# Turning a query tile's maxima into rows of the key product: four small products and one wide step, or one product and four narrow steps

## The chip, the cores and the metric

The kernel runs on one core of a Trainium2 chip. Its time is the device time of one execution in microseconds (us); several executions are timed and their median is compared. The core has TensorE (PE, matrix products; PEld is its weight load), VectorE (DVE), ScalarE (ACT), GpSimd (POOL) and SyncE (SP, which here only issues transfers). Each engine takes its instructions in order; semaphores tie the engines together.

## The reference

One step of a decoder trunk for a prompt of 2048 tokens and 8 samples of 4 tokens. Both share the weights. A layer is a normalisation, one wide input projection, an attention branch (A), a gated recurrence (B), a gated merge of both, an output projection and a residual. The change lies in branch A of the prompt, which attends in three ways: to 127 compressed blocks, to the 8 best blocks of 64 keys, and to a window of 512 keys. For the selected blocks and the window:

```
ss = einsum('bgrtd,bgtnsd->bgrtns', qg, ksg) + bias_s      # selected
ps = masked_softmax(ss, ms)
sw = einsum('bgrtd,blgd->bgrtl', qg, kw) + table[:, :, t5_bucket(rel_w)]
o_win = einsum('bgrtl,blgd->bgrtd', masked_softmax(sw, mw), vw)
```

There are 2 key heads (g) with 4 query heads (r) each. A softmax may subtract any number per query and head before the exponential; the kernel subtracts a maximum, so that the exponential stays in range. The bias differs from key to key only within some 112 positions of the query; beyond that it is one value.

## The kernel before

Everything up to about 1430 us is projections, compression, the samples' attention and the recurrence. `attention_setup` then builds constants, and `prompt_phase` runs the prompt's attention and, beside it, the remaining projections (`pfill`) and the merge with its output projection (`block`, handed out in small parts by `fill`).

The prompt's queries are cut in 16 tiles of 128. `run_block` takes one tile at a time in the order `ORDER`. A unit is a tile and a key head. Logits are computed transposed, 128 keys by 4 x 128 queries, by `score`: two or more products into one PSUM tile `st` (L1633, biases at L1639 and L1640 or L1642, and L1643). The maximum has to be subtracted along the queries, so it is put into extra rows of the query operand `qs` (rows 96 on) that meet constant rows of the key operand `kas` or `kw`. `probs` then takes the exponential twice on ScalarE (L1432 in 32 bits, L1433 in 16 bits), GpSimd takes their difference (L1434), and `pv` multiplies with the values (L1440, L1441, L1443). While one tile is attended to, the maxima of the next one are found (`max_ops`) and the compressed part of the one after (`prep`).

`max_ops` computes the untransposed logits of up to 4 key tiles per PSUM tile `mx` (L1518), adds the near bias by products with a flipped identity (L1520), one for the query's own key tile (128 columns) and one for the tile before it (112 columns), adds the window's far edge in the same way, and reduces over the keys on VectorE (L1521). `last` reduces over the chunks and, after the selected branch, calls `neg_row`.

`neg_row` takes maxima as 128 queries x 4 heads x n (n is 2 for selected and window together, 1 for the compressed branch), splits them in two 16-bit halves in `xd` (L1420, L1421), turns each head's 2n columns into 2n rows by a product with the identity into its quarter of the PSUM tile `tr` (L1424, four products of 128 columns), and writes all 4 x 128 queries in one ScalarE step with a bias per row (L1426). It is called once per unit for the selected branch (out `qs`) and once for the compressed branch (out `qc`): 64 calls, 4 for each query tile. `tr` has one buffer, which `sel` (L1584) and `finish` (L1660) use too.

The order of the work is written out in `run_block`: lists A (maxima of the next tile) and B (compressed part of the one after) are spread over the key tiles of the present one, and `fill` adds merge work by credit. Tile's scheduler then plans each engine's order from the dependencies and its own timeline (`TC_ARGS`). The first two tiles' compressed parts and the first tile's maxima are done ahead of the loop, from about 1430 us on, between pieces of `pfill`; this stretch is called the lead-in below.

Of the kernel before, what the change touches and what calls it, by code (L numbers as in the profile page):

```python
# [10 lines left out]
F32 = mybir.dt.float32  # L11
# [42 lines left out]
def shape_constants():  # L54
# [46 lines left out]
    c["shift"] = (np.arange(256)[None, :] + np.arange(16)[:, None] == 127).astype(np.float32)  # L101
    kb = np.zeros((36, 2048), np.float32)
    kb[:32] = (np.arange(2048)[None, :] // 64 == np.arange(32)[:, None]) * 2.0 ** 15
    kb[32:36:2] = 1024.0
    c["kblk"] = kb
    wone = np.zeros((36, 256), np.float32)
    wone[33::2] = 1024.0
    c["wone"] = wone
    c["edge"] = np.where(rows[:, None] > rows[None, :], 0.0, -60000.0).astype(np.float32)
    c["edgeq"] = c["edge"].T.copy()  # L110
# [18 lines left out]
def trunk_kernel(ctx: ExitStack, tc: tile.TileContext, A, O):  # L129
# [1112 lines left out]
    def attention_setup(st, a):  # L1242

        pc_ = st.enter_context(tc.tile_pool(name="pc", bufs=1, side="right"))
        with tc.tile_pool(name="ps0", bufs=2, side="right") as p0, tc.tile_pool(name="ps0p", bufs=1, space=PSUM, side="right") as p0p:
# [28 lines left out]
            ve.tensor_mul(swb, swb, tw)  # L1274
            nb = con.tile([4, 2], F32, name="nb")
            ve.memset(nb, LN_P * QS / 1024)
            for n in (1, 2):
                ve.memset(nb[:n, n - 1:n], 0.0)
            ve.tensor_scalar(gates[:, :16], gates[:, :16], vsc, None, op0=OP.mult)
            a.update(nb=nb, sk=sk, sv=sv, vsc=vsc, swa=swa, swb=swb, swo=swo, u2=u2)  # L1280

# [33 lines left out]
            t_ = p0.tile([128, 512], F32, name="cl")  # L1315
            sy.dma_start(t_[64:100, :256], A["c_wone"])
            a["wone"] = pc_.tile([100, 256], F16, name="wone")
            ve.tensor_copy(a["wone"][64:100], t_[64:100, :256])

# [6 lines left out]
            for g in range(2):  # L1326
                h0 = g * 4 * 2 * BRN
                for dl in range(2):
# [9 lines left out]
                    tq = pc_.tile([128, 4, 128], F16, name=f"tq{g}{dl}")  # L1338
                    ve.tensor_copy(tq, rq)
                    a["TQ"][g, dl] = tq  # L1340
# [13 lines left out]
            for g in range(2):  # L1354
                ka = pc_.tile([98, 128], F16, name=f"kac{g}0")
                k2 = pc_.tile([98, 128], F16, name=f"kac{g}1")
                kb = pc_.tile([128, 128], F16, name=f"kbc{g}")
                ve.tensor_scalar(ka[:64], kcp[:, g], sk[:64], None, op0=OP.mult)
                ve.memset(ka[96:98], 1024.0)
                ve.tensor_copy(k2[:64], ka[:64])  # L1360
                ve.memset(k2[96:98], 1024.0)
# [13 lines left out]
            for g in range(2):  # L1375
                KA["s", g] = pc_.tile([100, NP], F16, name=f"kas{g}")
                KB["s", g] = pc_.tile([128, NP], F16, name=f"kbs{g}")
            V["s"] = pc_.tile([128, 16, 2, 129], F16, name="vs16")
            ve.memset(V["s"][:, :, :, 64:65], 1.0)
            for c in range(4):  # L1380
                cs = slice(c * 512, (c + 1) * 512)
                bl = p0.tile([100, 512], F32, name="bl")
                sy.dma_start(bl[64:100], A["c_kblk"][:, cs])
                for g in range(2):
                    ka, kb = KA["s", g], KB["s", g]
                    kr = p0.tile([128, 512], F32, name="qr")
                    for h in range(2):
                        sy.dma_start(kr[h * 64:(h + 1) * 64], ks_d[g * 64:(g + 1) * 64, cs])
                    ac.activation(kb[:, cs], kr, AF.Copy, scale=sk)
                    ve.tensor_copy(ka[:64, cs], kb[:64, cs])  # L1390
                    ve.scalar_tensor_tensor(kb[:64, cs], kr[:64], sk[:64], ka[:64, cs], op0=OP.mult, op1=OP.subtract)
                    ve.tensor_copy(ka[64:100, cs], bl[64:100])
# [13 lines left out]
    def prompt_phase(a, st, pfill, state, sw):  # L1406
# [9 lines left out]
        def neg_row(m, dst):  # L1416

            n = m.shape[2]
            x = pu.tile([128, 4, 4], F16, name="xd")[:, :, :2 * n]
            ve.tensor_scalar(x[:, :, :n], m, -1.0 / 1024, None, op0=OP.mult)  # L1420
            ve.scalar_tensor_tensor(x[:, :, n:], m, -1.0 / 1024, x[:, :, :n], op0=OP.mult, op1=OP.subtract)  # L1421
            pt = ptr.tile([128, 4, 128], F32, name="tr")
            for r in range(4):
                mm(pt[:2 * n, r], x[:, r], a["id"], r == 0, True)  # L1424

            ac.activation(dst, pt[:2 * n], AF.Identity, bias=a["nb"][:2 * n, n - 1:n], scale=1.0 / QS)  # L1426

# [20 lines left out]
        def window(c):  # L1448
            cs = slice(c * 256, (c + 1) * 256)
            for g in range(2):  # L1450
                kr = pu.tile([128, 256], F32, name="kr", bufs=1)
                for h in range(2):
                    sy.dma_start(kr[h * 64:(h + 1) * 64], kw_d[g * 64:(g + 1) * 64, cs])
                ka = pu.tile([100, 256], F16, name=f"kw{g}", bufs=4)
# [4 lines left out]
                ve.tensor_copy(ka[64:100], a["wone"][64:100])  # L1459
                KW[c, g], KX[c, g] = ka, kb  # L1460
# [16 lines left out]
        def loads(t, g, turn):  # L1477
            u = {"k": KA["c", g][turn]}
            q0 = t * 128
            for nm, n in (("s", 100), ("c", 98), ("b", 128)):  # L1480
                u[nm] = pu.tile([n, 4, 128], F16, name="q" + nm, bufs={"c": 2}.get(nm, 6))
# [6 lines left out]
        def max_ops(u, br, t, g):  # L1488

            qq, K, k0 = u["s"], 96, 0 if br == "s" else max(0, t - 4)  # L1490
            nt = t + 1 - k0
            nch = (nt + 3) // 4
            mp_ = pu.tile([128, 4, 4], F32, name="mp" + br, bufs=3)
# [3 lines left out]
            def one(c, r):  # L1497
                ka, kz = k0 + c * 4, min(k0 + c * 4 + 4, t + 1)
                n = (kz - ka) * 128
                pm = pmx.tile([128, 4, 128], F32, name="mx")  # L1500
                pmf = flat(pm)
                sp_ = []
                for kt in (t, t - 1):
                    if ka <= kt < kz:
                        w0 = 0 if kt == t else 129 - FAR
                        sp_.append((a["flip"], TQ[g, t - kt][:, r, w0:], kt - ka, w0))
                if br == "w" and t >= 4 and ka <= t - 4 < kz:
                    sp_.append((a["id"], a["edgeq"], t - 4 - ka, 0))
                if br == "s":
# [7 lines left out]
                for i, (x, y, kk) in enumerate(runs):  # L1517
                    mm(pmf[:, (x - ka) * 128:(y - ka) * 128], qq[:K, r], kk, i == 0, not sp_)  # L1518
                for i, (l, rr, kk, w0) in enumerate(sp_):
                    mm(pm[:, kk, w0:], l, rr, False, i == len(sp_) - 1)  # L1520
                ve.tensor_reduce(mp_[:, r, c:c + 1], pmf[:, :n], axis=AX.X, op=OP.max)  # L1521

            def last():
                ve.tensor_reduce(u["m"][:, :, "sw".index(br)], mp_[:, :, :nch], axis=AX.X, op=OP.max)
                if br == "s":
                    neg_row(u["m"], u["s"][96:100])

# [13 lines left out]
        def prep(u, t, g):  # L1541
# [44 lines left out]

            return [cmax, lambda: neg_row(X["m"][:, :, None], u["c"][96:98]), cs, cpv, sel]

# [429 lines left out]
```

## Time and profile before

| | |
|---|---|
| runs shown | 2498.12, 2499.87, 2505.35 us, median 2499.87 |
| the profiled execution's own time | 2498.46 us |
| its span in the trace | 2496.1 us |
| instructions | 57172, of these 22228 products and as many weight loads |

The profile is of one execution. A row of a timeline gives the start, the time taken, the engine, the line and what is written from what; "x4" stands for several in a row that were merged, and the idle time before with what ended it stands in brackets. The time from one start to the next on PE is what a product costs in a stream; the time of one product includes its way through the array. ACT, DVE and POOL rows give what one instruction takes.

### The profile page before, as it was taken

The page shows a single profiled execution, that of the slowest core. Times are in us where ns is not written, and L with a number is a line of the kernel's source. Part 1 is how long each engine was busy: PE and PEld are TensorE (multiplying, and loading weights), DVE is VectorE, ACT ScalarE, POOL GpSimd, SP SyncE. Part 2 cuts the span into 40 slices and gives each one's busy share as a digit, 9 for nine tenths or more (in the row PEclk, how much of TensorE's full clock was granted, in tenths as well). Part 3 has the DMA queues.
Part 4 walks back from the last instruction along what each step waited for, and adds up shares of the span by engine and source line. Part 5 has one row for each costly group of instructions (what it writes and reads, how often), then busy time and mean ns, then how long its engine had stood idle before and what let it go on. Part 6 is the DMA issues. An engine that isn't in the chain of part 4 may idle for free.

```text
span 2496.1 us, 57172 instructions
## 1 busy us (share of the span) xinstructions
PE 2357.9 (94%) x22228; PEld 1554.0 (62%) x22228; DVE 1575.8 (63%) x4232; ACT 1198.0 (48%) x2639; POOL 989.9 (40%) x1179
## 2 busy tenths in 40 slices
PE   5999999998999999999989969899999999999998
PEld 4988675554785555555555446656666666565765
DVE  7556455656325688777763667677777767767543
ACT  5544333422223366555552346436555666667763
POOL 0100102332102255444550006536656666677864
PEclk9999999999999999999999979999999999999999
DMA  6543314656322434333323652322222221211121
GB/s 202 170 121 115 121 69 163 218 205 217 131 65 105 144 105 132 115 118 97 109 87 98 192 159 63 79 81 69 78 58 72 57 66 51 63 52 45 48 59 46
DMA packets 266719, 264.96 MB, mean 106 GB/s; under 512 B 95100, under 2 KB 237872, under 8 KB 259280
## 3 DMA queue, kind: packets, MB, share of 16 engines
q1 hardware_dynamic: 257936, 223.56, 29.0%
q0 software_dynamic: 8512, 37.75, 4.6%
q8 instruction: 175, 2.87, 0.5%
q14 instruction: 96, 0.79, 0.1%
HBM read 181.84 MB, written 83.55 MB: 106 GB/s over the span
## 4 chain that ended last, share of the span: by engine, by line
PE 68%; DVE 14%; DMA 7%; ACT 4%; issue 4%; POOL 1%; SPq 1%; DVEq 0%; ACTq 0%; POOLq 0%
PE ps L361 14%; PE ps L440 9%; PE ps L1786 7%; PE ps L1754 6%; PE ps L421 4%; PE st L1643 3%; PE st L1633 3%; PE mx L1518 3%; DVE X L683 2%; DMA wraw<-in_w_in_dram 2%; PE ph L920 2%; PE po L1440 2%; PE po L1443 2%; PE po L1441 2%; DVE mps L1521 1%
## 5 line engine op out<-in xcount | busy, mean ns | idle before, releaser
L1434 POOL TENSOR_TENSOR Pl<-P,Ph 128x512 f16<-128x512 f32 (+5 forms) x444 | 516.6, 1173 | 406.8 <-ACT Ph L1433 171.6
L1432 ACT ACTIVATE P<-st 128x512 f32<-128x512 f32 (+3 forms) x444 | 264.6, 596 | 204.8 <-PE st L1643 157.5
L361 PEld LDWEIGHTS <-wh 128*128 128x128 f16 x2240 | 214.3, 99 | 190.4 <-issue 45.2
L1433 ACT ACTIVATE Ph<-st 128x512 f16<-128x512 f32 (+5 forms) x444 | 262.6, 593 | 14.9 <-PE po L1441 10.8
L361 PE MATMUL ps<-xh,wh 128*128 128x512 f16 (+1 forms) x1120 | 234.5, 344 | 11.0 <-DVE row L374 5.1
L1521 DVE TENSOR_REDUCE mps<-mx 128x1 f32<-128x512 f32 (+3 forms) x320 | 189.2, 605 | 75.9 <-PE mx L1518 45.7
L361 PE MATMUL ps<-xl,wh 128*128 128x512 f16 (+1 forms) x1120 | 236.0, 347 | 1.1 <-issue 1.0
L361 PE MATMUL ps<-xh,wl 128*128 128x512 f16 (+1 forms) x1120 | 232.3, 341 | 0.0
L440 PE MATMUL ps<-wh,xh 128*128 128x256 f16 (+3 forms) x680 | 189.4, 279 | 7.0 <-ACT to L447 4.3
L440 PE MATMUL ps<-wh,xl 128*128 128x256 f16 (+3 forms) x680 | 188.4, 278 | 4.0 <-DVE xl L327 4.0
L440 PE MATMUL ps<-wl,xh 128*128 128x256 f16 (+3 forms) x680 | 189.0, 278 | 0.0
L1440 PEld LDWEIGHTS <-Ph 128*128 128x128 f16 (+5 forms) x1776 | 138.8, 98 | 41.3 <-issue 6.9
L361 PEld LDWEIGHTS <-wl 128*128 128x128 f16 x1120 | 107.9, 98 | 86.3 <-issue 9.4
L1441 PEld LDWEIGHTS <-Ph 128*128 128x128 f16 (+5 forms) x1776 | 128.7, 96 | 32.7 <-issue 1.4
L440 PEld LDWEIGHTS <-xh 128*128 128x128 f16 (+1 forms) x1360 | 129.9, 99 | 30.7 <-issue 6.5
L686 POOL TENSOR_TENSOR X<-X,kt 128x128 f32<-128x128 f32 x160 | 81.8, 512 | 142.8 <-ACT X L685 142.8
L1521 DVE TENSOR_REDUCE mpw<-mx 128x1 f32<-128x512 f32 (+3 forms) x224 | 104.9, 485 | 49.6 <-PE mx L1520 46.7
L652 POOL TENSOR_TENSOR Xo<-Xo,qt 128x256 f32<-128x256 f32 x32 | 30.5, 953 | 260.4 <-ACT Xo L651 229.3
L1754 PEld LDWEIGHTS <-xh 128*128 128x128 f16 x1280 | 105.3, 98 | 30.3 <-issue 9.1
L1518 PE MATMUL mx<-kas,qs 96*128 96x512 f16 (+3 forms) x320 | 109.8, 355 | 10.4 <-DVE mps L1521 7.7
L1443 PEld LDWEIGHTS <-Pl 128*128 128x128 f16 (+3 forms) x1776 | 96.1, 97 | 30.9 <-POOL Pl L1434 8.4
L1440 PE MATMUL po<-vs,Ph 128*128 128x65 f16 x1088 | 106.6, 192 | 0.8 <-DVE otmp L1535 0.8
(538 smaller groups left out, 5918.9 us busy)
## 6 DMA issues: line engine op xcount, KB each, us to landing
wraw<-in_w_in_dram SPq DMA_DIRECT2D x22, 1024.0 KB
xt<-in_x_prompt_dram SPq DMA_DIRECT2D x32, 512.0 KB
ma_d<-row SPq DMA_DIRECT2D x8, 1040.0 KB
out_y_prompt_dram<-xt SPq DMA_DIRECT2D x16, 512.0 KB
sg<-ma_d SPq DMA_DIRECT2D x56, 128.0 KB
sg<-mb_d SPq DMA_DIRECT2D x56, 128.0 KB
mb_d<-row SPq DMA_DIRECT2D x18, 256.0 KB
q_d<-row SPq DMA_DIRECT2D x4, 1040.0 KB
```

Source lines behind the costliest of these rows:

```text
L361: mm(ps, l[:, kc], xs(r, t0, n)[:, kc], k == 0, k == 23)
L440: mm(ps, xs(l, t0, r)[:, kc], w[:, kc], k == 0, k == 23)
L1432: ac.activation(P[:n], ps, AF.Exp, scale=1.0 / QS)
L1433: ac.activation(ph[:n], ps, AF.Exp, scale=1.0 / QS)
L1434: sub.tensor_sub(pl[:n], P[:n], ph[:n])
L1440: mm(po[:, r, :w], ph[:n, rs[r]], v[:n, :w], first and r == 0, False)
L1441: mm(po[:, r, :64], ph[:n, rs[r]], v[:n, w:w + 64], False, False)
L1443: mm(po[:, r, :w], pl[:n, rs[r]], v[:n, :w], False, last)
L1518: mm(pmf[:, (x - ka) * 128:(y - ka) * 128], qq[:K, r], kk, i == 0, not sp_)
L1521: ve.tensor_reduce(mp_[:, r, c:c + 1], pmf[:, :n], axis=AX.X, op=OP.max)
L1754: mm(X["ps"], w[:, kc, cs], os_[o][:, kc], k == 0, k == 11)
L1786: mm(X["ps"], X["y"][y][:, kc, i0:i0 + r], W["o", kc // 4][w][:, kc % 4, cs], k == 0, k == 23)
```

## The change

The four products of `neg_row` become one: `xd` is laid out head by head, all 8n columns are turned into 8n rows at once, and each head has its own 2n of these rows, separate from the other heads'. The query operand gets 4 x 2n rows in place of 2n (`qs` 96 to 112, `qc` 96 to 104); in the 128 queries of head r only head r's rows hold numbers and the others are zero. Four ScalarE steps write them, one per head, each reading all 8n rows and taking a scale and a bias per row from the constant `own` (zero for rows of other heads). The key operands get matching constant rows (`c_kblk`, `c_wone`, the `memset` of `kac`). `own` comes by one transfer in place of three `memset`s of `nb`.

In `max_ops` the two bias tiles `tq` of a key head become one tile of 240 columns, and the two products with the flipped identity become one, over the last 240 columns. For that the chunks are cut so that a query's own key tile and the one before it always lie in one chunk: where a tile would have stood alone at the end it now takes the one before with it, and the five window tiles are cut as 3 and 2 or 2 and 3 in place of 4 and 1. The number of chunks stays.

```diff
-            x = pu.tile([128, 4, 4], F16, name="xd")[:, :, :2 * n]
-            ve.tensor_scalar(x[:, :, :n], m, -1.0 / 1024, None, op0=OP.mult)
-            ve.scalar_tensor_tensor(x[:, :, n:], m, -1.0 / 1024, x[:, :, :n], op0=OP.mult, op1=OP.subtract)
-            pt = ptr.tile([128, 4, 128], F32, name="tr")
+            x = pu.tile([128, 16], F16, name="xd")[:, :8 * n]
+            xv = x.rearrange("p (r k) -> p r k", r=4)
+            ve.tensor_scalar(xv[:, :, :n], m, -1.0 / 1024, None, op0=OP.mult)
+            ve.scalar_tensor_tensor(xv[:, :, n:], m, -1.0 / 1024, xv[:, :, :n], op0=OP.mult, op1=OP.subtract)
+            pt = ptr.tile([128, 4, 128], F32, name="tr")[:8 * n, 0]
+            mm(pt, x, a["id"], True, True)
+            own = a["own"][:8 * n, 2 - n]
             for r in range(4):
-                mm(pt[:2 * n, r], x[:, r], a["id"], r == 0, True)
-
-            ac.activation(dst, pt[:2 * n], AF.Identity, bias=a["nb"][:2 * n, n - 1:n], scale=1.0 / QS)
+                ac.activation(dst[:, r], pt, AF.Identity, bias=own[:, 4 + r:5 + r], scale=own[:, r:r + 1])
...
-            nch = (nt + 3) // 4
+            cut = [min(x, t - 1) for x in range(k0 + 4, t + 1, 4)]
+            if br == "w" and cut:
+                cut = [t - 1 - (t - 1) % 2]
+            cut = [k0, *cut, t + 1]
+            nch = len(cut) - 1
...
-                ka, kz = k0 + c * 4, min(k0 + c * 4 + 4, t + 1)
+                ka, kz = cut[c:c + 2]
...
-                for kt in (t, t - 1):
-                    if ka <= kt < kz:
-                        w0 = 0 if kt == t else 129 - FAR
-                        sp_.append((a["flip"], TQ[g, t - kt][:, r, w0:], kt - ka, w0))
-                if br == "w" and t >= 4 and ka <= t - 4 < kz:
-                    sp_.append((a["id"], a["edgeq"], t - 4 - ka, 0))
+                if kz > t:
+                    w = 127 + FAR if t else 128
+                    sp_.append((a["flip"], TQ[g][:, r, 127 + FAR - w:], n - w, n))
+                if br == "w" and t >= 4 and ka == t - 4:
+                    sp_.append((a["id"], a["edgeq"], 0, 128))
...
-            nb = con.tile([4, 2], F32, name="nb")
-            ve.memset(nb, LN_P * QS / 1024)
-            for n in (1, 2):
-                ve.memset(nb[:n, n - 1:n], 0.0)
+            own = con.tile([16, 2, 8], F32, name="own")
+            sy.dma_start(own.rearrange("p i r -> p (i r)"), A["c_own"])
...
-                    neg_row(u["m"], u["s"][96:100])
+                    neg_row(u["m"], u["s"][96:112])
...
-            return [cmax, lambda: neg_row(X["m"][:, :, None], u["c"][96:98]), cs, cpv, sel]
+            return [cmax, lambda: neg_row(X["m"][:, :, None], u["c"][96:104]), cs, cpv, sel]
```

## Rows read from the trace of the kernel before

**Rows 1.** First part of the page: busy us, share of the span, instructions.

```profile
PE 2357.9 (94%) x22228; PEld 1554.0 (62%) x22228; DVE 1575.8 (63%) x4232; ACT 1198.0 (48%) x2639; POOL 989.9 (40%) x1179
```

**Rows 2.** Windows, two stretches: length, busy us (instructions) per engine, clock, DMA, GB/s.

```profile
1430.00:1600.00 170.00, 138.71 (x1487) 87.51 (x1486) 116.89 (x395) 85.92 (x157) 66.62 (x71) 0.88 0.38 103
1600.00:2400.00 800.00, 782.21 (x8646) 522.65 (x8645) 560.07 (x1498) 472.04 (x919) 509.63 (x493) 0.98 0.22 62
```

**Rows 3.** Timeline of PE, two places in a dense stretch.

```profile
2079.87 0.27 PE L1520 MATMUL mx<-tq,h_flip 128*128 128x128 f16 x2
2079.98 0.19 PE L1440 MATMUL po<-vs,Ph 128*128 128x65 f16 x1
...
2315.31 0.39 PE L1424 MATMUL tr<-h_id,xd 128*4 128x128 f16 x4
2315.63 0.40 PE L1518 MATMUL mx<-kw,qs 96*128 96x128 f16 x3
```

**Rows 4.** Lines L1520 and L1424, ns min/median/max; the last from 1600 to 2400 alone.

```profile
L1520 PEld LDWEIGHTS <-h_flip x496: 95/98/152, 1475.0 to 2382.4; 128*128 128x128 f16 x166
L1424 PEld LDWEIGHTS <-xd x256: 79/83/129, 1438.8 to 2389.2; 128*2 128x2 f16 x64, 128*4 128x4 f16 x64
...
L1424 PE MATMUL tr<-h_id,xd x192: 217/218/314, 1601.8 to 2389.2; 128*4 128x128 f16 x104, 128*2 128x128 f16 x88
```

**Rows 5.** Groups of ACT by shape: count, busy us, mean ns, idle before, releaser.

```profile
L1432 ACT ACTIVATE P<-st 128x512 f32<-128x512 f32 x412 | 245.7, 596 | 189.5 <-PE st L1643 157.5 <-POOL Pl L1434 23.9 <-PE po L1443 2.3
L1763 ACT ACTIVATE yh<-pr 128x256 f16<-128x256 f32 x56 | 23.4, 417 | 36.4 <-POOL pr L1761 36.2
L1426 ACT ACTIVATE qs<-tr,nb 4x512 f16<-4x512 f32 x32 | 21.7, 677 | 61.4 <-PE tr L1424 61.1
L748 ACT ACTIVATE jk<-ov 128x128 bf16<-128x128 f32 x64 | 16.9, 275 | 0.0
L1456 ACT ACTIVATE kx<-kr,sk 128x256 f16<-128x256 f32 x16 | 8.1, 506 | 14.2 <-DMA kr<-kw_d 12.4 <-PE st L1633 1.7
```

**Rows 6.** Timeline of ACT where one query tile gives way to the next.

```profile
1892.37 0.68 ACT L1426 ACTIVATE qs<-tr,nb 4x512 f16<-4x512 f32 x1 [7.44 <-PE tr L1424]
1893.94 0.68 ACT L1426 ACTIVATE qs<-tr,nb 4x512 f16<-4x512 f32 x1 [0.90 <-PE tr L1424]
1894.65 0.60 ACT L1432 ACTIVATE P<-st 128x512 f32<-128x512 f32 x1
1895.14 0.59 ACT L1433 ACTIVATE Ph<-st 128x512 f16<-128x512 f32 x1
```

**Rows 7.** Timeline of PE at the same place.

```profile
1891.75 0.58 PE L1424 MATMUL tr<-h_id,xd 128*4 128x128 f16 x4
...
1893.32 0.58 PE L1424 MATMUL tr<-h_id,xd 128*4 128x128 f16 x4
1893.84 1.03 PE L1643 MATMUL st<-qs,kw 100*128 100x512 f16 x2
...
1896.72 0.19 PE L1440 MATMUL po<-vw,Ph 128*128 128x65 f16 x1
```

**Rows 8.** Windows: ahead of this place, round it, and round the last like it.

```profile
1665.00:1885.00 220.00, 218.04 (x2432) 146.40 (x2431) 162.94 (x457) 130.91 (x256) 140.54 (x138) 1.00 0.26 71
1885.00:1900.00 15.00, 13.13 (x124) 8.85 (x122) 12.62 (x37) 6.08 (x12) 5.89 (x6) 0.77 0.35 109
...
2160.00:2175.00 15.00, 13.25 (x109) 8.34 (x106) 12.87 (x34) 5.67 (x11) 4.76 (x6) 0.77 0.08 19
```

**Rows 9.** Waits of the whole program, PE: us in total, times, longest.

```profile
PE mx L1518 <- DVE mpw L1521: 8.6, 10, 1.8
PE mx L1518 <- DVE mps L1521: 8.3, 18, 2.4
```

**Rows 10.** Groups of DVE by shape, the reductions over one chunk.

```profile
L1521 DVE TENSOR_REDUCE mpw<-mx 128x1 f32<-128x512 f32 x104 | 69.9, 685 | 12.6 <-PE mx L1520 12.0
L1521 DVE TENSOR_REDUCE mpw<-mx 128x1 f32<-128x128 f32 x104 | 27.7, 287 | 36.5 <-PE mx L1520 34.3 <-PE po L1443 1.4
```

More of the change, by code (lines that the diff above doesn't have):

```diff
@@ L101, in shape_constants @@
     c["shift"] = (np.arange(256)[None, :] + np.arange(16)[:, None] == 127).astype(np.float32)
-    kb = np.zeros((36, 2048), np.float32)
+    kb = np.zeros((48, 2048), np.float32)
     kb[:32] = (np.arange(2048)[None, :] // 64 == np.arange(32)[:, None]) * 2.0 ** 15
-    kb[32:36:2] = 1024.0
+    kb[32::2] = 1024.0
     c["kblk"] = kb
-    wone = np.zeros((36, 256), np.float32)
+    wone = np.zeros((48, 256), np.float32)
     wone[33::2] = 1024.0
     c["wone"] = wone
+    own = np.zeros((16, 2, 8), np.float32)
+    for i, n in enumerate((2, 1)):
+        p = np.arange(8 * n)
+        own[:8 * n, i, :4] = (p[:, None] // (2 * n) == np.arange(4)[None, :]) / QS
+        own[:8 * n, i, 4:] = own[:8 * n, i, :4] * (p // n % 2)[:, None] * (LN_P * QS / 1024 * QS)
+    c["own"] = own.reshape(16, 16)
     c["edge"] = np.where(rows[:, None] > rows[None, :], 0.0, -60000.0).astype(np.float32)
@@ L1274, in attention_setup @@
             ve.tensor_mul(swb, swb, tw)
-            nb = con.tile([4, 2], F32, name="nb")
-            ve.memset(nb, LN_P * QS / 1024)
-            for n in (1, 2):
-                ve.memset(nb[:n, n - 1:n], 0.0)
+            own = con.tile([16, 2, 8], F32, name="own")
+            sy.dma_start(own.rearrange("p i r -> p (i r)"), A["c_own"])
             ve.tensor_scalar(gates[:, :16], gates[:, :16], vsc, None, op0=OP.mult)
-            a.update(nb=nb, sk=sk, sv=sv, vsc=vsc, swa=swa, swb=swb, swo=swo, u2=u2)
+            a.update(own=own, sk=sk, sv=sv, vsc=vsc, swa=swa, swb=swb, swo=swo, u2=u2)
             OSh = p0.tile([64, 8, 32], F16, name="OSh", bufs=1)
@@ L1315, in attention_setup @@
             t_ = p0.tile([128, 512], F32, name="cl")
-            sy.dma_start(t_[64:100, :256], A["c_wone"])
-            a["wone"] = pc_.tile([100, 256], F16, name="wone")
-            ve.tensor_copy(a["wone"][64:100], t_[64:100, :256])
+            sy.dma_start(t_[64:112, :256], A["c_wone"])
+            a["wone"] = pc_.tile([112, 256], F16, name="wone")
+            ve.tensor_copy(a["wone"][64:112], t_[64:112, :256])
             brt = br_d.tensor
@@ L1327, in attention_setup @@
                 h0 = g * 4 * 2 * BRN
+                tq = a["TQ"][g] = pc_.tile([128, 4, 127 + FAR], F16, name=f"tq{g}")
                 for dl in range(2):
@@ L1337, in attention_setup @@
                     sy.dma_start(rq, toep(h0 + BRN + (BRN - 1 - BR0) - 127 - 128 * dl, [[1, 128], [2 * BRN, 4], [1, 128]]))
-                    tq = pc_.tile([128, 4, 128], F16, name=f"tq{g}{dl}")
-                    ve.tensor_copy(tq, rq)
-                    a["TQ"][g, dl] = tq
+                    if dl:
+                        ve.tensor_copy(tq[:, :, :FAR - 1], rq[:, :, 129 - FAR:])
+                    else:
+                        ve.tensor_copy(tq[:, :, FAR - 1:], rq)
                     yield
@@ L1354, in attention_setup @@
             for g in range(2):
-                ka = pc_.tile([98, 128], F16, name=f"kac{g}0")
-                k2 = pc_.tile([98, 128], F16, name=f"kac{g}1")
+                ka = pc_.tile([104, 128], F16, name=f"kac{g}0")
+                k2 = pc_.tile([104, 128], F16, name=f"kac{g}1")
                 kb = pc_.tile([128, 128], F16, name=f"kbc{g}")
                 ve.tensor_scalar(ka[:64], kcp[:, g], sk[:64], None, op0=OP.mult)
-                ve.memset(ka[96:98], 1024.0)
+                ve.memset(ka[96:104], 1024.0)
                 ve.tensor_copy(k2[:64], ka[:64])
-                ve.memset(k2[96:98], 1024.0)
+                ve.memset(k2[96:104], 1024.0)
                 ve.scalar_tensor_tensor(kb[:64], kcp[:, g], sk[:64], ka[:64], op0=OP.mult, op1=OP.subtract)
@@ L1375, in attention_setup @@
             for g in range(2):
-                KA["s", g] = pc_.tile([100, NP], F16, name=f"kas{g}")
+                KA["s", g] = pc_.tile([112, NP], F16, name=f"kas{g}")
                 KB["s", g] = pc_.tile([128, NP], F16, name=f"kbs{g}")
@@ L1381, in attention_setup @@
                 cs = slice(c * 512, (c + 1) * 512)
-                bl = p0.tile([100, 512], F32, name="bl")
-                sy.dma_start(bl[64:100], A["c_kblk"][:, cs])
+                bl = p0.tile([112, 512], F32, name="bl")
+                sy.dma_start(bl[64:112], A["c_kblk"][:, cs])
                 for g in range(2):
@@ L1391, in attention_setup @@
                     ve.scalar_tensor_tensor(kb[:64, cs], kr[:64], sk[:64], ka[:64, cs], op0=OP.mult, op1=OP.subtract)
-                    ve.tensor_copy(ka[64:100, cs], bl[64:100])
+                    ve.tensor_copy(ka[64:112, cs], bl[64:112])
                     yield
@@ L1453, in window @@
                     sy.dma_start(kr[h * 64:(h + 1) * 64], kw_d[g * 64:(g + 1) * 64, cs])
-                ka = pu.tile([100, 256], F16, name=f"kw{g}", bufs=4)
+                ka = pu.tile([112, 256], F16, name=f"kw{g}", bufs=4)
                 kb = pu.tile([128, 256], F16, name=f"kx{g}", bufs=4)
@@ L1458, in window @@
                 ve.scalar_tensor_tensor(kb[:64], kr[:64], a["sk"][:64], ka[:64], op0=OP.mult, op1=OP.subtract)
-                ve.tensor_copy(ka[64:100], a["wone"][64:100])
+                ve.tensor_copy(ka[64:112], a["wone"][64:112])
                 KW[c, g], KX[c, g] = ka, kb
@@ L1479, in loads @@
             q0 = t * 128
-            for nm, n in (("s", 100), ("c", 98), ("b", 128)):
+            for nm, n in (("s", 112), ("c", 104), ("b", 128)):
                 u[nm] = pu.tile([n, 4, 128], F16, name="q" + nm, bufs={"c": 2}.get(nm, 6))
@@ L1518, in one @@
                     mm(pmf[:, (x - ka) * 128:(y - ka) * 128], qq[:K, r], kk, i == 0, not sp_)
-                for i, (l, rr, kk, w0) in enumerate(sp_):
-                    mm(pm[:, kk, w0:], l, rr, False, i == len(sp_) - 1)
+                for i, (l, rr, x, y) in enumerate(sp_):
+                    mm(pmf[:, x:y], l, rr, False, i == len(sp_) - 1)
                 ve.tensor_reduce(mp_[:, r, c:c + 1], pmf[:, :n], axis=AX.X, op=OP.max)
```

## The prediction

> **What bounds the kernel now.** I read the page's first part, then windows by stage, the groups by shape of the instructions touched, and timelines of places where a tile's maxima become rows. TensorE (PE) is busy for 94% of the span [rows 1]. The changed code runs only behind 1430 us, in two kinds of time [rows 2]. From 1600 to 2400 us PE is busy for 782 of 800 us, with a granted clock of 0.98: here a product less is time saved, and a longer step on another engine costs only where PE runs out of other work. From 1430 to 1600 us, the lead-in, PE is busy for 139 of 170 us: here chains through VectorE, ScalarE and transfers set the pace.
>
> The dense stretch isn't even. From 1665 to 1885 us PE is busy for 218 of 220 us at clock 1.00. Round 1892 us it is busy for 13.1 of 15 us at a mean clock of 0.77, so part of it at the lower of two levels, while VectorE is busy for 12.6 [rows 8]. There a query tile ends, the timeline has no product of the merge, and ScalarE stands idle for 7.4 us until the product of `neg_row` releases it [rows 6]. Three more changes of tile look like this one, the last round 2168 us [rows 8]. At these four a longer `neg_row` has least to hide behind.
>
> **The change part by part, in us.**
>
> *One product for four.* In the dense stretch the four take 0.32 from the first start to the next line's start [rows 3]. Two flipped products of 128 and 112 columns take 0.11 in the same stretch, so 128 columns cost about 0.055. Three products less save 0.165. 192 of the 256 products, 48 calls, lie behind 1600 [rows 4]: 48 x 0.165 = 7.9 saved. Bounds: the four cost 0.10 more than their columns; if that went too, 0.265 a call, 12.7. Where PE waits anyway the saving is nothing. I take 7.9, since the narrow weights that come with the 0.10 stay, 16 wide in place of 4.
>
> *One flipped product for two.* 240 per run of the program go (15 tiles, 2 heads, 2 branches, 4 query heads; 496 weight loads [rows 4] become 256). The columns stay: 240 x 0.055/128 is 0.103 against 0.11. 240 x 0.007 = 1.7 saved, bounds 0 and the rival below.
>
> *The cuts.* A window row's reductions took 685 ns (512 columns) and 287 (128) [rows 10], 1.04 a column. 384 and 256 columns are 554 and 420 by that: 972 before, 974 behind. VectorE's load stays; nothing, bounds in the rivals.
>
> *Four ScalarE steps for one.* No row shows a step with 128 columns and both scale and bias from a tile, so I build it. The old step took 677 ns with 512 columns [rows 5]. A column costs (596 - 275)/384 = 0.836 ns, from L1432 and L748, so 384 fewer leave 356. A scale taken from a tile costs 506 - 417 = 89 more (L1456 against L1763): 445. Then the queue: P and Ph overlap, Ph starts 0.49 behind P though P takes 0.60, but the old step overlaps with nothing: P starts at 1894.65, 0.03 behind its end [rows 6]. It writes from partition 96 on as the new ones do, so I give each 24 ns more: 4 x 0.469 = 1.88 against 0.70, 1.18 more a call. Bounds: four steps of 275 that overlap by 0.10 cost 0.70, nothing more; four of 506 with the gap cost 2.12, 1.42 more. The sum over 64 calls is 76 us of ScalarE, busy for 472 of 800 in the dense stretch; as load that fits, so it counts only as lateness.
>
> The Trainium skill (page "ScalarE: Activation LUTs", section "What ACT_TABLE_LOAD costs") gives 186 ns plus 0.833 a column, some 93 for each scale or bias from a tile, and says that steps back to back overlap by about 93. By that page four steps are an estimated 1.64 us. Its slope agrees with the 0.836 here; its overlap does not with L1426's 0.03 gap, and the row decides. By the page a call adds 0.94 and not 1.18, and the lateness below is some 1.5 less in all.
>
> *Lateness at the four bare changes of tile.* Taken from 1892 [rows 6, 7], where the clock's lower level (1.2 of 2.4 GHz) makes 128 columns twice 0.055, 0.11. The first ScalarE step starts 0.62 behind the first product; three products less make that 0.29, so the four run from 1892.04 to 1893.92, where the one ended at 1893.05. `tr` has one buffer: the second head's product, at 1893.32 now, waits until some 1893.94, and PE's queue stands behind it. The scores (L1643) started 0.52 behind it, now 0.19: 1894.13, 0.29 later than now. The second head's steps run from 1894.23 to 1896.11, and P starts at 1896.13 in place of 1894.65, 1.48 late. Ph ended at 1895.73 and PE took it at 1896.72: 0.99 is cover. Left are 0.49, with the 0.29 in them: 4 x 0.49 = 2.0 lost. Bounds: 0 if P is planned between the two calls, 4 x 1.5 = 6.0 if the cover is used up elsewhere.
>
> *Lateness at the other changes of tile and in the compressed branch.* Their two calls lie further apart than one call now lasts, so one call's 1.18 falls on a tile, less 0.165 that the product ends sooner: 1.0 against a cover of 0.99. I take 1.0 in all, bounds 0 and 40 x 1.0.
>
> *Lead-in.* 16 calls, while PE lies idle for 31 of 170 us [rows 2]. That is a fifth of the time, so I let three calls (a fifth) show in full, 1.0 each as above: 3.0. Bounds 0 and 16.
>
> *Setup.* One small transfer for three memsets and 12 more constant rows, beside PE's projections: nothing.
>
> Sum: -7.9 - 1.7 + 2.0 + 1.0 + 3.0 = -3.6, which makes the profiled execution's 2498.46 some 2494.9. The median of the runs lies 1.4 above that execution, so the forecast is 2496.3, 0.14% less than 2499.87. What this kernel's runs can tell from no change is about 0.3%, 7.5 us: 2492.4 to 2507.4 counts as the same.
>
> **The rivals.**
>
> *Slower: `tr`'s single buffer.* The place is every change of tile, not four. PE stands behind the second head's product, P behind eight ScalarE steps instead of two. With no cover, 15 changes cost 1.5 each, 22.5, and the lead-in 3.0; less 9.6 saved that is +15.9, 2515.8; with 0.4 of cover at each it is 15 x 1.1 + 3.0 - 9.6 = +9.9, 2509.8. It decides for slower from 0.94 a change on, (7.5 + 9.6 - 3.0)/15. For it: ScalarE's idle rows at L1426, 61.1 us in all [rows 5], say that it often comes last. Against: PE has 218 of 220 us of work around most of them [rows 8].
>
> *Faster: PE stops waiting for VectorE.* L1518 waits 16.9 us for reductions [rows 9], since `mx` has two buffers. Chunks of 2 and 3 instead of 4 and 1 might free buffers more evenly: half of it, 8.4, on top of 9.6 with the lateness hidden, gives 2499.9 - 18.0 = 2481.9. Against: VectorE's sum is the same, and where it is the bound an even cut gives nothing.
>
> *Faster: weight loads set PE's pace.* Loads of 98 and 83 ns [rows 4] would go with each product: 240 x 0.098 + 192 x 0.083 = 39.5, less 6.0 lateness: 2466.4. Against: two flipped products with two loads took 0.11 [rows 3], less than 0.196; loads overlap.
> The Trainium skill (page "TensorE: Matmul & The Clock Gate", section "Back-to-back issue gap") states about 81 ns for a 128-column product with its load in a real stream, which points the same way; 0.055 here speaks against it.
>
> *The change doesn't do what it says*: the planner could put the four steps apart, with other work between, so that the rows are complete later still. It ends as the first rival and is counted there.
>
> **How the numbers follow.** Forecast 0.49, between 2489 and 2505 by itself; `tr` and its like 0.25, even VectorE 0.22, weight loads 0.04. The faster rivals make 0.26 faster, the first rival 0.25 slower, and 0.49 is within 0.3%. The range for 8 in 10 reaches into both sides: down to 2484, where 6.3 of the 8.4 us of waits for VectorE are gone, and up to 2511, just past the slower rival with 0.4 of cover; this leaves out about 1 in 10 at either end.
>
> **What would show it.** L1424 with 64 products and L1520 with 352 (256 flipped, 96 edges); PE's product count lower by some 430 to 480. L1426 with 256 steps of about 445 ns, the four 0.47 apart and without overlap; at 300 ns or with overlap the ScalarE term is wrong. The second L1424 at the four changes of tile 2.2 or more behind the first, with PE idle ahead of it and ACT's `tr` as releaser; if the pair stands as before, the lateness is wrong. L1518's wait for L1521 still near 17 us; if it is halved, the second rival has it. ScalarE's busy time up by 70 us with PE's idle time in 1600 to 2400 unchanged within 5 us shows that the load was hidden. Wrong would be any change beyond 7.5 us.

## The result, and the profile after

The changed kernel takes 2523.04 us (median of 6 runs, 2515.94 to 2526.09) against 2501.27 us of the kernel before on the same chip (6 runs, 2495.87 to 2509.05): 1.0086 of its time, 95% interval 1.0071 to 1.01. The forecast was 2496.3 us and no change that can be told; it is slower, and outside the range.

The profiled execution took 2524.28 us, its span 2522.2. First the engines' part of the page, in the form of [rows 1]:

```profile
PE 2359.4 (94%) x21748; PEld 1546.1 (61%) x21748; DVE 1558.8 (62%) x4229; ACT 1247.1 (49%) x2831; POOL 993.8 (39%) x1179
```

TensorE has 480 products fewer, of which the forecast's sum counted 432 (the other 48 are key products of the maxima, L1532, that the new cuts save), and is busy for 1.5 us longer. The windows show where, in the columns of [rows 2]:

```profile
1430.00:1600.00 170.00, 131.52 (x1321) 79.07 (x1320) 102.27 (x364) 95.29 (x201) 65.06 (x69) 0.86 0.35 98
1600.00:2400.00 800.00, 768.03 (x8117) 507.33 (x8116) 547.64 (x1508) 495.61 (x1036) 502.62 (x483) 0.97 0.21 61
2400.00:2522.00 122.00, 108.99 (x1237) 72.72 (x1234) 45.01 (x139) 58.99 (x129) 65.26 (x69) 0.95 0.17 50
```

From 1600 to 2400 TensorE does 8117 products where it did 8646, and is idle for 32 us instead of 18. So the work is not heavier; it is done more slowly, and what isn't done by 2400 is done behind it.

The groups by shape (the view of [rows 5] and [rows 10], behind 1430 us) of the new product, the new steps and the even window cuts:

```profile
L1535 DVE TENSOR_REDUCE mpw<-mx 128x1 f32<-128x384 f32 x104 | 55.9, 550 | 44.2 <-PE mx L1534 43.8
...
L1436 ACT ACTIVATE qs<-tr,own 16x128 f16<-16x128 f32 x128 | 47.4, 438 | 48.4 <-PE tr L1433 48.1
L1436 ACT ACTIVATE qc<-tr,own 8x128 f16<-8x128 f32 x128 | 47.3, 438 | 3.2 <-PE tr L1433 2.5
...
L1535 DVE TENSOR_REDUCE mpw<-mx 128x1 f32<-128x256 f32 x104 | 42.2, 417 | 18.4 <-PE mx L1534 17.5
...
L1433 PE MATMUL tr<-h_id,xd 128*16 128x128 f16 x32 | 7.5, 233 | 1.1 <-DVE qs L1599 0.4 <-ACT qs L1436 0.2 <-DVE oo L1686 0.2
L1433 PE MATMUL tr<-h_id,xd 128*8 128x128 f16 x32 | 7.2, 225 | 3.1 <-ACT qc L1436 2.0 <-DVE qs L1599 1.2
```

A step takes 438 ns (forecast 445) and a reduction 550 and 417 (554 and 420). Then the change of tile of [rows 6], now at 1907 us; the timeline of ScalarE:

```profile
1907.20 1.48 ACT L1436 ACTIVATE qs<-tr,own 16x128 f16<-16x128 f32 x4 [8.49 <-PE tr L1433]
1909.04 1.48 ACT L1436 ACTIVATE qs<-tr,own 16x128 f16<-16x128 f32 x4 [0.35 <-PE tr L1433]
1910.54 0.60 ACT L1442 ACTIVATE P<-st 128x512 f32<-128x512 f32 x1
```

and of all engines, in excerpt:

```profile
1906.89 0.28 PE L1433 MATMUL tr<-h_id,xd 128*16 128x128 f16 x1
...
1908.73 0.27 PE L1433 MATMUL tr<-h_id,xd 128*16 128x128 f16 x1
1908.93 1.03 PE L1657 MATMUL st<-qs,kw 112*128 112x512 f16 x2
```

Four steps last 1.48 us, not 1.88: 4 x 0.438 is 1.75, so they overlap by 0.09 each. The second product starts 0.05 behind the first head's last step (1907.20 + 1.48 = 1908.68): `tr`'s one buffer holds it, as forecast, 1.84 behind the first product where [rows 7] have 1.57 and the forecast had 2.19. P starts 3.65 behind the first product where it started 2.90 behind in [rows 6, 7], 0.75 late and not 1.48. TensorE's waits for reductions over the whole program (us, times, longest), against [rows 9]:

```profile
PE mx L1532 <- DVE mpw L1535: 12.7, 23, 2.3
PE mx L1532 <- DVE mps L1535: 8.8, 19, 1.3
...
```

The forecast's local terms are thus near or too dear, and yet the time is 27 us above it. Where it went is seen when the trace is cut at the changes of tile: between the first head's row products at every second change (number 0 opens the first tile, number j gives way from the j-th tile in order to the next), in us, worked out from the starts in the traces (the kernels e7 to e13 are explained below):

| stretch | before | after | own order (e11) | first job held (e12) | pair jobs held (e13) | all held (e7) | before, late (e8) |
|---|---|---|---|---|---|---|---|
| start to 0 | 1500.3 | 1499.6 | 1503.2 | 1497.1 | 1503.6 | 1495.6 | 1501.4 |
| 0 to 2 | 70.9 | 74.2 | 75.2 | 71.7 | 74.6 | 71.9 | 71.2 |
| 2 to 4 | 88.1 | 86.6 | 87.2 | 87.7 | 87.6 | 87.8 | 86.9 |
| 4 to 6 | 109.6 | 118.5 | 117.9 | 118.5 | 105.6 | 105.5 | 105.3 |
| 6 to 8 | 123.0 | 128.1 | 124.1 | 125.4 | 128.0 | 128.5 | 128.0 |
| 8 to 14 | 420.9 | 427.1 | 423.6 | 420.7 | 420.0 | 420.9 | 419.3 |
| 14 to end | 183.5 | 188.2 | 186.0 | 185.5 | 185.2 | 182.5 | 181.5 |

Each column is one traced execution. That of e7 is the fastest of its 11 runs, 7 us under their median, so its column flatters it.

Fourteen of the 26 us between the two spans are lost from change 4 to change 8. There the whole stretch reads, in the kernel before,

```profile
1659.00:1892.00 233.00, 229.15 (x2520) 153.35 (x2519) 175.56 (x495) 134.97 (x263) 144.38 (x141) 0.98 0.26 73
```

and after:

```profile
1660.00:1907.00 247.00, 235.87 (x2391) 153.70 (x2390) 169.50 (x499) 146.62 (x311) 146.33 (x141) 0.96 0.25 71
```

The same tiles, the same 576 products of merge and out-projection (counted in the traces between the two changes), 129 products fewer in all, 14 us longer: 7 of them idle (11.1 against 3.9), 7 in products that take longer at a lower mean clock. The rest of this text asks why. One thing differs that no step of the forecast moved. A planner orders each engine's instructions. TensorE's filler, the steps of the gate merge and the out-projection, comes from jobs: the first of 64 steps, then one for each pair of tiles. In the planned order of before the last eight steps of the first job stand behind the 17th and 18th score product (L1633, in order), after behind the 9th to 12th. Steps 215 to 223 (the end of the pair job ahead of change 6) stand behind the 84th, after behind the 77th to 80th. The merge products in two stretches ahead of change 1 show it (length, then PE and PEld busy and count, clock, DMA); before:

```profile
1500.00:1520.00 20.00, 4.96 (x119) 4.19 (x116) 0.91 0.25 64
1520.00:1540.00 20.00, 2.48 (x49) 2.06 (x49) 1.00 0.31 76
```

and after, where the job is over by 1534:

```profile
1500.00:1520.00 20.00, 3.66 (x93) 3.49 (x89) 0.92 0.29 74
1520.00:1540.00 20.00, 0.00 (x0) 0.00 (x0) 1.00 0.11 26
```

Changes 1 and 6, which had 25 and 28 products of filler within 6 us, now have none.

### The profile page after: what moved, and what is told of

Read it like the earlier page. It is cut to its first block, busy times and chain, and to the rows that moved or that the text cites. A ratio compares the mean times of both kernels' runs of the same rounds, so it can differ in the third digit from the quotient of the medians.

```text
span 2522.2 us, 56422 instructions
## 1 busy us (share of the span) xinstructions
PE 2359.4 (94%) x21748; PEld 1546.1 (61%) x21748; DVE 1558.8 (62%) x4229; ACT 1247.1 (49%) x2831; POOL 993.8 (39%) x1179
## 4 chain that ended last, share of the span: by engine, by line
PE 67%; DVE 14%; DMA 7%; ACT 5%; issue 4%; POOL 1%; SPq 1%; DVEq 0%; ACTq 0%; POOLq 0%
PE ps L369 15%; PE ps L448 9%; PE ps L1800 7%; PE ps L1768 7%; PE ps L429 3%; PE st L1657 3%; PE st L1647 3%; PE mx L1532 3%; DVE X L691 2%; PE ph L928 2%; DMA wraw<-in_w_in_dram 2%; PE po L1450 2%; PE po L1453 2%; PE po L1451 2%; PE pt L911 1%
## 5 line engine op out<-in xcount | busy, mean ns | idle before, releaser
L1444 POOL TENSOR_TENSOR Pl<-P,Ph 128x512 f16<-128x512 f32 (+4 forms) x444 | 519.9, 1181 | 428.7 <-ACT Ph L1443 181.9
L1443 ACT ACTIVATE Ph<-st 128x512 f16<-128x512 f32 (+4 forms) x444 | 262.7, 594 | 9.3 <-PE po L1451 6.8
L1450 PEld LDWEIGHTS <-Ph 128*128 128x128 f16 (+6 forms) x1776 | 140.3, 99 | 51.1 <-ACT Ph L1443 7.5
L1451 PEld LDWEIGHTS <-Ph 128*128 128x128 f16 (+6 forms) x1776 | 130.3, 97 | 35.4 <-issue 3.3
L1535 DVE TENSOR_REDUCE mpw<-mx 128x1 f32<-128x384 f32 (+3 forms) x224 | 105.5, 484 | 63.1 <-PE mx L1534 61.5
L1453 PEld LDWEIGHTS <-Pl 128*128 128x128 f16 (+5 forms) x1776 | 98.6, 97 | 33.8 <-POOL Pl L1444 7.7
L1532 PE MATMUL mx<-kas,qs 96*128 96x512 f16 (+3 forms) x320 | 108.8, 353 | 8.9 <-DVE mps L1535 7.6
## 6 DMA issues: line engine op xcount, KB each, us to landing
sg<-ma_d SPq DMA_DIRECT2D x56, 128.0 KB
sg<-mb_d SPq DMA_DIRECT2D x56, 128.0 KB
```

The lines of the kernel that those rows point to most:

```text
L1443: ac.activation(ph[:n], ps, AF.Exp, scale=1.0 / QS)
L1444: sub.tensor_sub(pl[:n], P[:n], ph[:n])
L1450: mm(po[:, r, :w], ph[:n, rs[r]], v[:n, :w], first and r == 0, False)
L1451: mm(po[:, r, :64], ph[:n, rs[r]], v[:n, w:w + 64], False, False)
L1453: mm(po[:, r, :w], pl[:n, rs[r]], v[:n, :w], False, last)
```

## The experiments

All ratios are to the kernel before on the same chip, with 95% intervals. The diffs of e1, e2, e4, e5 and e6 are against the changed kernel and show the core of the edit; those of e3 and n1 are against the kernel before, and n2 has n1's edit on the changed one. Theory A: ScalarE's longer steps and `tr` cost the time (D, in later runs, the same as a chain). B: the new cuts cost it. C: the planned order of the filler costs it.

**One half without the other.** `e1_rows` has the rows' product and the four steps, with the old chunks and two flipped products:

```diff
-            cut = [min(x, t - 1) for x in range(k0 + 4, t + 1, 4)]
...
+            nch = (nt + 3) // 4
...
```

> The neg_row half of the change alone: one product and four ScalarE steps, with the old chunks and two flipped products. The whole change lost 22 us where 3.6 were forecast as gain. Theory A, lateness of the four ScalarE steps (1.48 us from the first's start to the last's end in the changed kernel, 0.68 before) and the hold on tr: this half alone is 18 to 24 us slower than before. Theory B, the cuts: this half alone is 5 to 10 us faster, as its 192 products are saved and the cuts are not there. Theory C, the order that the planner gives the engines is new with any edit and itself worth some 20 us: anything between, and the losses of the two halves don't add up to 22.

Measured: 2518.09 us, 1.0102 (1.0079 to 1.0124), 23 us slower, as A gave too. `e2_cuts` has the new cuts and the one flipped product alone:

```diff
-            for r in range(4):
-                ac.activation(dst[:, r], pt, AF.Identity, bias=own[:, 4 + r:5 + r], scale=own[:, r:r + 1])
+            ac.activation(dst, pt[:2 * n], AF.Identity, bias=a["nb"][:2 * n, n - 1:n], scale=1.0 / QS)
...
```

> The max_ops half alone: new cuts, one flipped product for two, old neg_row with four products and one ScalarE step. Theory A: 0 to 3 us faster than before. Theory B: 20 to 30 us slower. Theory C: anything, not additive with the other half.

Measured: 2498.77 us, 1.0025 (1.0008 to 1.0041). B falls. The halves (1.02% and 0.25%) add up to more than the whole, 0.86%, though by little more than the intervals allow: two costs side by side would add up.

**ScalarE's steps alone, and without them.** `e3_four_four` is the kernel before with its one step cut in four:

```diff
-            ac.activation(dst, pt[:2 * n], AF.Identity, bias=..., scale=1.0 / QS)
+            for r in range(4):
+                ac.activation(dst[:, r], pt[:2 * n, r], AF.Identity, bias=..., scale=1.0 / QS)
```

> The kernel before with one edit: the one ScalarE step of neg_row is cut in four, one per head, each reading its 128 columns of the four products as before. No product saved, no wider rows. Theory A: 20 to 32 us slower than before, as the lateness is there and the saved products aren't. Theory B: within 3 us of before. Theory C: anything between.

Measured: 2503.84 us, 1.003 (1.0017 to 1.0044): four steps by themselves, in an order planned anew, cost about a third of the loss, and not A's 20 to 32 us. `e4_one_dve` is the whole change with one VectorE instruction in place of the four steps:

```diff
-            for r in range(4):
-                ac.activation(dst[:, r], pt, AF.Identity, bias=own[:, 4 + r:5 + r], scale=own[:, r:r + 1])
+            ve.scalar_tensor_tensor(dst, pt[:, None, :].to_broadcast([8 * n, 4, 128]), own[:, 4:5],
+                                    own[:, :4, None].to_broadcast([8 * n, 4, 128]), op0=OP.add, op1=OP.mult)
...
```

> The whole change, but the rows are spread by one VectorE step (add a bias per row, multiply by 1/QS or zero per row and head) over 512 columns instead of four ScalarE steps; about 0.7 us by the reductions over 512 columns. Theory A: the loss goes, 0 to 10 us faster than before. Theory B: still 15 to 25 us slower. Theory C: anything between.

Measured: 2513.66 us, 1.0074 (1.0054 to 1.0094). Its group by shape:

```profile
L1435 DVE SCALAR_TENSOR_TENSOR qs<-tr,own 16x512 f16<-16x512 f32 x32 | 23.8, 743 | 3.4 <-PE tr L1433 2.5
```

The rows are spread in 0.74 us, about as in the one old step of [rows 5] (677 ns), and most of the loss is there all the same. As the account of the whole loss, A falls. (The 64 steps are 48 us more work for VectorE; TensorE's waits for reductions are 23.2 us here and 21.5 in the changed kernel, so that is not where the loss comes from.)

**The planner off.** Both kernels with their instructions in the order in which the program writes them:

```diff
-TC_ARGS = {"schedule_with_timeline_sim": True}
+TC_ARGS = {}
```

> The kernel before with the planner's reordering off: each engine runs its instructions in the order in which the program writes them; the work is the same. Fillers (the gate-merge products) then stand at every change of tile, by the written order, where the planned order leaves four changes without. Theory C (the loss of the changed kernel comes from the order that the planner makes of it): this run alone decides nothing, its place is beside n2; estimate 2500 to 2560 us. Theory D (the loss comes from the chain itself: the later last row and the one buffer of tr): the same. What counts is the ratio of n2 to n1.

> The changed kernel with the planner's reordering off, in the order that the program writes. Theory C: without the planner the change is worth what its products give, so 0 to 10 us below n1 (ratio 0.996 to 1.000). Theory D: the chain of product, four ScalarE steps and tr's one buffer costs the same in the written order, so 15 to 25 us above n1 (ratio 1.006 to 1.010).

Measured: 2541.92 us, 1.0183 (1.0164 to 1.0201), for the kernel before, and 2541.75 us, 1.0179 (1.0159 to 1.0199), for the changed one. In the written order no gain or loss can be told; runs of the changed one reach from 2530.93 to 2544.79.

**Four equal products, another PSUM pool.** `e5_four_same` writes the new product four times, each step reading its own:

```diff
-            mm(pt, x, a["id"], True, True)
+            for r in range(4):
+                mm(pt[:, r], x, a["id"], r == 0, True)
...
```

> The whole change, but the one product is written four times, into four stretches of tr, and each ScalarE step reads its own; the work of TensorE is that of before again (192 products more), the plan leaves the changes 1 and 2 without filler and the change 6 with 4 gate-merge products. Theory C: plan and time stay near the changed kernel's, 2515 to 2530 us. Theory E (TensorE falls to its lower clock because it has fewer products): back to within 5 us of before. Theory D: 2520 to 2535, the product ending later.

Measured: 2512.9 us, 1.0065 (1.0048 to 1.0082). 192 products more than the changed kernel, and not slower: taking them away is not what made the changed kernel slow, and E, back to within 5 us, falls. `e6_mx` takes the product's PSUM tile from the maxima's pool:

```diff
-            pt = ptr.tile([128, 4, 128], F32, name="tr")[:8 * n, 0]
+            pt = pmx.tile([128, 4, 128], F32, name="mx")[:8 * n, 0]
```

> The whole change, but the rows' product is written to a tile of the maxima's PSUM pool (two buffers) and not to tr (one). Theory D: the second head's product no longer waits for the first head's last step, and the other users of tr are not held, so most of the loss goes: 2497 to 2510 us. Theory C: the order is planned anew, but stays without filler at the changes: 2512 to 2528 us.

Measured: 2542.55 us, 1.0186 (1.0169 to 1.0203), worse than either theory gave. TensorE's waits of this kernel, as above:

```profile
PE mx L1532 <- DVE mpw L1535: 14.3, 19, 2.5
PE mx L1532 <- DVE mps L1535: 11.1, 18, 2.4
...
PE mx L1433 <- DVE xd L1431: 7.6, 10, 1.2
```

The waits for reductions are 25.4 us against 21.5, and the rows' product waits for its own operand `xd`. The run gives D no support, but the pool got another user and the order was planned anew, so it doesn't weigh `tr`'s buffer by itself.

**The filler held.** In the next runs nothing of the work changes, and the planner still orders the rest. Each filler step gets an edge of order alone: on TensorE it is issued behind a given score product and a given row product. `HOLD` lists the pair for each of the 752 steps; it is read off a planned order. (The dots stand for the kind of edge, one of order alone.)

```diff
+    def held(ins):
+        s_, q_ = HOLD[len(PT)]
+        PT.append(ins)
+        for l, k in ((SC, s_), (QN, q_)):
+            k = min(k, len(l))
+            if k:
+                tc.add_manual_dep(ins.ins, l[k - 1].ins.name, ..., reason="hold")
```

`e7_after_held`: the changed kernel, `HOLD` from the planned order of the kernel before.

> The whole change, and nothing of its work altered; but each gate-merge and out-projection step is held on TensorE behind the same score product and the same call of the rows' function as in the planned order of the kernel before (an edge of order alone, no wait for a result). In the plan the changes of tile 1 and 6 then have 19 and 33 gate-merge products within 40 products, where the changed kernel has none. Theory C (the loss is that the plan spends the filler early, so that two more changes of tile run bare): the loss goes, 2490 to 2505 us. Theory D (the loss is the longer chain of product and four steps, and tr's one buffer): 2510 to 2522 us.

Measured: 2501.96 us, 1.0013 (1.0002 to 1.0024). The longer chain and `tr`'s one buffer are all there, and the loss is gone but for 0.13%. `e11_after_own`: the same edges from the changed kernel's own planned order.

> The whole change with the same kind of edges as in e7, but from the changed kernel's own planned order, so that the fillers stay about where they are in it (none at the changes of tile 1 and 6). Theory C (it is where the filler stands): as the changed kernel, ratio 1.006 to 1.010, 2512 to 2524 us. Theory F (edges as such, by fixing the order of TensorE, give the gain of e7): near e7, ratio 0.999 to 1.003.

Measured: 2518.6 us, 1.0074 (1.0057 to 1.0091). Edges as such give nothing (F falls); where the filler stands, with what the planner moves along with it, does. That is little: of TensorE's other products behind 1430 us, counted in the traces, half stand at most 1 place elsewhere in e7 than in e11 and nine in ten at most 10. Between the changed kernel and e11 it is 0 and 5 places, and these two take the same time within their intervals. The stretch from change 4 to 8 in e7 and e11, held as before,

```profile
1655.00:1889.50 234.50, 227.54 (x2389) 150.37 (x2388) 171.91 (x499) 147.37 (x311) 143.77 (x141) 0.98 0.26 72
```

and by its own order:

```profile
1665.50:1907.50 242.00, 231.30 (x2386) 151.97 (x2384) 167.42 (x490) 147.23 (x311) 145.92 (x141) 0.97 0.25 71
```

Equal work, 7.5 us apart: as between before and after, half of it idle time (10.7 against 7.0) and half products that take longer, at a mean clock of 0.97 against 0.98.

**Which job.** The edges of e7 on the first job's 64 steps alone, and on all others alone:

> The whole change with the edges of e7 on the first merge job alone (its 64 steps before the second change of tile); the other jobs as planned. Theory C, if a step spent early costs alike everywhere: a quarter of the gain at most, ratio 1.005 to 1.008. Theory G (the lead-in's chains are the place of the loss): most of the gain, ratio 1.000 to 1.004.

Measured: 2510.29 us, 1.0033 (1.0021 to 1.0045).

> The whole change with the edges of e7 on all jobs but the first. Theory C, alike everywhere: most of the gain, ratio 1.001 to 1.004. Theory G: little of it, ratio 1.005 to 1.009.

Measured: 2505.49 us, 1.0023 (1.0012 to 1.0034). Each gives back more than half of e11's loss, 0.41 and 0.51 points of 0.74; together they give 0.61. The table's columns show the place: against e11 the first job's edges win 3.5 us from change 0 to 2 (and 6 ahead of it, where traces with this part in the same order lie up to 4 apart), the others' 12 us between 4 and 6, of which 4 are lost again between 6 and 8. G as an exclusive cause falls, and so does "alike everywhere".

**A bare change by itself.** `e8_before_bare` is the kernel before with its own order held, but the 30 steps at changes 1 and 6 moved to 4 to 6 score products behind them.

> The kernel before with the same edges of order, by its own plan, except that the steps that stood at the changes of tile 1 and 6 (16 and 14 of them) are held until 4 to 6 score products after them. The work is that of before. Theory C: the two changes run bare and cost what they cost in the changed kernel beyond before, some 5 and 10 us: 2503 to 2514 us. Theory D: within 5 us of before.

Measured: 2497.49 us, 0.9991 (0.9978 to 1.0004). C's first form, that a bare change as such costs 5 to 10 us, is not borne out. The run doesn't price it cleanly: within 6 us of changes 2, 4 and 8, which had no filler in before, e8's trace has 9, 3 and 11 products of it, and 7 are left at change 6. Windows of 15 us at change 6 show the difference; after, and then e8:

```profile
1775.00:1790.00 15.00, 12.50 (x97) 7.00 (x97) 11.36 (x45) 9.51 (x22) 5.93 (x6) 0.77 0.27 76
```

```profile
1761.00:1776.00 15.00, 12.66 (x132) 8.15 (x130) 13.03 (x40) 9.06 (x17) 7.41 (x7) 1.00 0.28 75
```

Both have TensorE idle for some 2.4 us. But after has the mean clock at 0.77 and does 97 products, e8 has it at 1.00 and does 132 (some of its products are the small ones that the change saves). In e7 the same change has its filler:

```profile
1757.00:1772.00 15.00, 15.00 (x95) 7.47 (x94) 9.71 (x39) 7.70 (x20) 3.00 (x3) 1.00 0.18 70
```

**Filler kept for the other bare changes.** The last eight steps ahead of the changes 2, 4, 8, 10, 12 and 14 are kept for the change itself (two ahead of the first row product, three behind each), in the kernel before and in the changed one:

> The kernel before with the same edges, except that the last eight steps ahead of each change of tile that is bare in it (2, 4, 8, 10, 12, 14) are kept for the change: two ahead of the first call of the rows' function, three behind it, three behind the second. Theory C: a bare change holds some 8 us of idle and half-clock time, 48 us in six; with eight steps of 0.43 to 0.64 us each in it a third of that goes, 8 to 16 us: 2480 to 2490 us. Theory D: within 5 us of before.

Measured: 2490.76 us, 0.9955 (0.9941 to 0.9969).

> The whole change, with the edges of e7 and the eight steps of e9 kept for the six bare changes. Theory C: e7 less the gain of e9, and by its fewer products at or under e9: 2474 to 2492 us. Theory D: 2500 to 2515 us.

Measured: 2488.26 us, 0.9954 (0.994 to 0.9967). The dense stretch of e10 in the columns of [rows 2]:

```profile
1600.00:2400.00 800.00, 781.21 (x8434) 517.59 (x8432) 563.91 (x1519) 517.18 (x1083) 522.08 (x501) 0.99 0.22 64
```

Both beat the kernel before and the changed one, and they are equal: with the filler well placed, the change itself is worth nothing that can be measured here, to some 5 us either way.

## Why the prediction was wrong

*The step that failed* stands in the first part: "a longer step on another engine costs only where PE runs out of other work". It took where that other work stands from the trace of before, and so did every term behind it: the four bare changes, the 0.99 of cover, the 1.0 for all other changes. The change had the whole order planned anew. TensorE's filler came earlier, and the places where TensorE runs out moved: e7 against e11 is 0.61 points, where the whole loss is 0.86, on the same work. The prediction knew the planner only as something that might put the four steps apart. A term for a new order, bounded from both sides, is missing, so it stood at nothing without a reason; the kernel before with and without its planned order (1.83% apart) shows how far such a term can reach.

*One product for four, one flipped for two* (-9.6): the instructions went, the time didn't. With the old order back (e7), the stretch from change 4 to 8 has TensorE busy for 1.6 us less than before (227.5 against 229.2) and idle for 3.1 more (7.0 against 3.9). e5, with the products back, is no slower. So the saving didn't reach the time; whether those products were off the path, or the longer steps gave the saved time back as idle time, no run tells, since none has the one without the other in a held order. The bound's 0.10 beyond the columns was one place's: from 1600 to 2400 the four products start 55 ns apart at the median, as other products of 128 columns do (58 ns between two of L1520).

*Four ScalarE steps*: the size of one was right (438 for 445 ns), the queueing wrong. I read from [rows 6] that a step writing from partition 96 on overlaps with nothing; that holds between it and P (1909.04 + 1.48 = 1910.52, P at 1910.54), not among the four. The Trainium skill (page "ScalarE: Activation LUTs", section "What ACT_TABLE_LOAD costs") had the overlap of some 93 ns, and this trace agrees with 0.09; the 1.64 us worked out from that page was too dear all the same, as 1.48 was measured. I had let the row decide for a case that it didn't show. The added time per call is 0.80 and not 1.18.

*Lateness at bare changes*: right in kind (second product held by `tr`, scores behind it), 0.75 late and not 1.48 at the one worked out. The trace of before has six changes without filler within 6 us (2, 4, 8, 10, 12, 14) and not four. Even at 0.75 each, 4.5 us, it is small beside what the order did.

*Other changes, compressed branch, lead-in* (1.0 and 3.0): the stretch ahead of change 0 is no longer than before (1499.6 against 1500.3); the first term no run weighs by itself.

*The cuts*: VectorE's load stayed, as costed. Waits of L1532 for reductions rose from 16.9 [rows 9] to 21.5 us, so the second rival, half of them gone, is out.

*The slower rival* gave 2515.8 by `tr`'s buffer at every change. The sign is right and the cause isn't: e7 has that buffer and costs 0.13%, so the hold on `tr` by itself doesn't make the loss. *Weight loads*: 480 fewer, and nothing gained.

*With the order kept*, the forecast's -3.6 us is compared by three pairs: written order -0.2 us (n2, n1), spread filler within 0.01 points (e10, e9), the order of before +0.13 points (e7; 0.02 to 0.24). All are inside 0.3%. The first two are uncertain by some 5 us and don't exclude -3.6; e7 does. So the sign of the sum is not borne out.

*Open.* Why the planner hands out filler earlier in the changed kernel was not tried one cause at a time. e1 and e5 share it at both changes (0 products within 6 us of change 1, 5 and 4 of change 6), e5 without the saved products; e4, without the ScalarE steps, has 20 at change 1 and none at 6. And bareness by itself doesn't set the price: e3 has none at change 1 and e2 only 3 at change 6, and they lose 0.30% and 0.25%. Why early filler costs most between 4 and 6 is seen only as idle time and lower clock; no single wait accounts for it.

## What to carry to other kernels

Where a planner orders the instructions, an edit of a few us can change the order of everything, and that may weigh more than the edit. Price it as a term of its own. Before blaming the edited instructions, run the edit in an order held fixed: the written one, or the old one by edges of order. Work that can be done at any time should be kept for the places where the engine has nothing else.

## What was not expected of the hardware

Four ScalarE steps that read one PSUM tile and write side by side from partition 96 on overlap by 0.09 us each (1.48 for 4 x 0.438). So do 191 pairs of such steps in the trace of after, while none of the 45 P that come right behind such a step starts before its end (0.01 us or more behind it). And equal idle time in TensorE can come with either clock: 12.5 of 15 us busy at a mean of 0.77 after, 12.66 of 15 at 1.00 in e8.
